# Where a seven-product feed-forward stage makes its weight sums, operand sums and squares

## The chip, the cores and the metric

The kernel runs on one core of a Trainium2 chip. The metric is the device time of one execution in microseconds (us); lower is better. Engines are named as in the profile: PE is TensorE, DVE is VectorE, ACT is ScalarE, POOL is GpSimd, SP is SyncE, which here only issues DMAs. All data is float32; a matmul operand is split into a high part (type fp32r) and a low part, so that one float32 product is three matmuls: high by high, high by low, low by high.

## What is computed

One step of a decoder trunk of two layers, for 512 prompt rows and 32 sample rows (NT = 544 columns; everything is kept transposed, features on partitions):

```python
for i in range(DEPTH):                     # DEPTH = 2, D_MODEL = 1024, D_FF = 2816
    x = x + 0.5 * swiglu(rmsnorm(x, norm_ff1[i]), ffn1_gate[i], ffn1_up[i], ffn1_down[i])
    x = x + (mlstm if i % 2 == 0 else chunk_mlp)(rmsnorm(x, norm_mix[i]))
    x = x + 0.5 * swiglu(rmsnorm(x, norm_ff2[i]), ffn2_gate[i], ffn2_up[i], ffn2_down[i])
y = rmsnorm(x, norm_final)

def swiglu(x, gate, up, down):
    return (silu(x @ gate) * (x @ up)) @ down
```

The states of the mLSTM (matrix memory, normaliser, stabiliser, convolution rows) and the chunk MLP's rows are outputs too. The change touches none of that.

## The kernel before, in words

The kernel has six stages in order: ffn1 of layer 0, the mLSTM, ffn2 of layer 0, ffn1 of layer 1, the chunk MLP, ffn2 of layer 1. The first and the last (`ffn_seven`, L565) work on 2x2 blocks with seven products in place of eight, in the manner of Strassen and Winograd; the other four are plain. The change is in the two seven-product stages and in what prepares their operand.

**Units.** A stage is a list of units (class `Unit`, L172). A unit is one 256-column slab of a weight matrix, stored as four blocks (12, 11, 21, 22). `gated(j)` makes two blocks of gate rows, `hidden(j)` two blocks of up rows and multiplies by the gate, `lowered(m, ...)` adds two rows of blocks of the down projection to x. The list is gated 0, hidden 0, gated 1, hidden 1, gated 2, hidden 2, gated 3, four lowered units over hidden 0 to 2, and so on in groups of three (`SV_GROUPS`, L48). Indices 0, 9 and 10 of gate and up (`EIGHT`, L49) and the last four lowered units have eight products and need no sums. A gated or hidden unit of seven products has 7 x 12 = 84 matmuls, a lowered one 63, each 128x128 by 128x272.

**Sums of weights.** The seven products need, besides blocks 11, 12 and 22, the sums called "7", "5", "6" and "3". "7" and "5" are made by accumulating DMAs that POOL issues onto loaded blocks (`u_add`, L421, parts "7" and "5"). "6" is "7" plus block 22, and "3" is "6" plus block 12 (tile rawd): two adds on POOL. `u_split` then makes high and low parts in halves "a" (12, 11), "b" (6, 7), "c" (5, 22) and "d" (3): ACT copies into the high part, DVE subtracts for the low part (`split_into`, L273). The raw loads rotate over six buffers, three a unit, so that the load of the unit after next takes the buffers of the unit at hand; high and low parts of "a" and "b" rotate over two, those of "c" and "d" have one each, and so has rawd.

**Sums of the operand.** The operand of gate and up (the scaled x; four pairs of row tiles) has eight blocks a pair: B11, B21, B22, B12 and four sums T4, T1, T2, T3. `sums_x` (L394) scales two tiles into tile hT (two ACT copies), splits the first four blocks, makes the sums on DVE (`sums`, L386) and splits those. `prep_sq` (L302) squares a tile of x on ACT and adds it to `acc` on POOL, for the RMS norm; `prep_end` (L312) sums acc over partitions on PE and makes rstd.

**What sets the order.** Within a seven-product stage `self.nc` is an `Ordered` wrapper (L166): on every engine the instructions keep the order in which the program issues them, so one that waits holds back all behind it on its engine. `u_run` (L477) is that order. With u the unit at hand, v the next, w the one after and p the one before, an iteration issues, for a unit of seven products:

- product 11 into bank 0 and ACT's negated copy into bank 2
- loads "a" and "b" of w on SP, the accumulating DMA "7" of w on POOL
- split "c" of u; load "c" of w; the accumulating DMA "5" of w
- the last product ("3") of p, then p's eviction on DVE
- product 12; split "d" of u (reads rawd); split "a" of v
- product 6; ACT's copy of bank 2 into bank 3; `p.then(0)` (ACT's Silu and POOL's product of the gate with rstd, or a part of the hidden split)
- product 7 and its copy to tile e; `p.then(1)`
- adds "6" of w and "3" of v on POOL; split "b" of v
- products 22 (into bank 2) and 5 (into bank 3), and ACT's copy of bank 3 into bank 1

The stage's front (L649 to L664) splits the first unit's weights and, in the first stage, prepares x pair by pair; in the last stage x is prepared by the loop of the chunk MLP's output projection (L1447), outside the Ordered wrapper. Unit 0 runs pair by pair (`wide`), and `prep_end` sits in its iteration.

## Time and profile before

| what | value |
|---|---|
| time, median of 3 runs | 2431.47 us (2431.13 to 2433.59) |
| the profiled execution's own time | 2430.62 us |
| its span, first to last instruction | 2428.9 us |
| PE busy | 2295.4 us (95%), 17504 matmuls |
| DVE busy | 1417.8 us (58%) |
| ACT busy | 958.5 us (39%) |
| POOL busy | 590.4 us (24%) |
| mean granted PE clock | 0.981 of full speed |
| HBM | 154 GB/s over the span |

Times in the rows count from the span's start. A busy share is an average over stages with different limits; matmuls overlap in the pipeline, so that a busy PE is not PE at its peak. The clock granted to PE has two levels, 1.2 and 2.4 GHz; a mean of 1.00 says that it was at the upper one throughout. "x <- y" behind a wait says what ended it. In the tables of instructions, a helper's line stands for all that it issues: in the two Ordered stages everything has L157 (the wrapper's call), so the names of the tiles tell operations apart: raw (loaded weights; on POOL the add "6" or the issue of an accumulating DMA), rawd (the add "3"), whi/wlo (halves "a" and "b"), whc/wlc ("c"), whd/wld ("d"), set (a unit's four banks), hT, xsh/xsl, s, acc, sq.

### The profile page before, as it was taken

The numbers are of one execution on the slowest core, as the hardware profiler recorded it, in microseconds if no ns is written. First come the engines' busy times: TensorE is split into PE (matmuls) and PEld (weight loads), VectorE is DVE, ScalarE is ACT, GpSimd is POOL, SyncE is SP. The second block draws the span as 40 slices with busy tenths as digits, with TensorE's granted clock in tenths as the row PEclk, the third lists the DMA queues.
The fourth block names the chain that finished last, engine by engine and source line by source line (L and its number), as shares of the span: only waits on it lengthen the run. The fifth ranks groups of instructions, "written<-read, shape, count | busy, mean of one in ns | idle before, by whom it ended". The sixth has DMA issues, their size and how long they took to land.

```text
span 2428.9 us, 42264 instructions
## 1 busy us (share of the span) xinstructions
PE 2295.4 (95%) x17504; PEld 2183.5 (90%) x17504; DVE 1417.8 (58%) x1909; ACT 958.5 (39%) x1410; POOL 590.4 (24%) x612
## 2 busy tenths in 40 slices
PE   6988899899999999999999999999999989888997
PEld 5888899888887888999999999999999988888897
DVE  5868685754436666745444455545344667677764
ACT  5535453343535444521222342222244444444443
POOL 3444431334201100210111121011120024444421
PEclk8999999999999999999999999999999999998998
DMA  4555553367676663448463445647232225555541
GB/s 137 137 137 137 138 141 110 112 196 231 206 275 225 222 228 127 155 152 280 165 207 124 128 153 167 242 156 237 84 114 80 72 74 127 130 144 132 149 121 53
DMA packets 158600, 376.85 MB, mean 155 GB/s; under 512 B 16224, under 2 KB 40624, under 8 KB 158408
## 3 DMA queue, kind: packets, MB, share of 16 engines
q1 hardware_dynamic: 112528, 289.66, 36.4%
q0 software_dynamic: 25328, 60.24, 11.5%
q10 hardware_dynamic: 20552, 24.26, 2.8%
q8 instruction: 137, 2.24, 0.4%
q14 instruction: 55, 0.45, 0.1%
HBM read 314.29 MB, written 59.81 MB: 154 GB/s over the span
## 4 chain that ended last, share of the span: by engine, by line
PE 74%; DVE 7%; issue 6%; POOL 6%; DMA 4%; ACT 2%; SPq 0%; POOLq 0%; ACTq 0%; DVEq 0%
PE mm L262 49%; PE set L157 13%; POOL raw L157 3%; DVE hT L157 2%; POOL rawd L157 2%; PE mm L1316 2%; PE s L1109 2%; PE s L1243 1%; PE s L1279 1%; DMA raw<-in_ffn_gate 1%; DMA raw<-in_ffn_up 1%; PE s L887 1%; PE s L262 1%; PE mm L700 1%; DVE wlc L157 1%
## 5 line engine op out<-in xcount | busy, mean ns | idle before, releaser
L276 ACT ACTIVATE whi<-raw 128x1024 fp32r<-128x1024 f32 (+2 forms) x216 | 221.9, 1027 | 751.1 <-PE mm L262 644.9
L262 PE MATMUL mm<-xgh,whi 128*128 128x272 f32 x2368 | 494.8, 290 | 0.2 <-DVE x L1350 0.2
L262 PE MATMUL mm<-xgl,whi 128*128 128x272 f32 x2368 | 490.2, 288 | 0.0
L262 PE MATMUL mm<-xgh,wlo 128*128 128x272 f32 x2368 | 489.8, 288 | 0.0
L262 PEld LDWEIGHTS mm<-xgh,whi 128*128 128x128 f32 x2368 | 372.1, 188 | 18.5 <-issue 14.5
L262 PEld LDWEIGHTS mm<-xgl,whi 128*128 128x128 f32 x2368 | 371.4, 188 | 0.4 <-DVE xgl L157 0.2
L262 PEld LDWEIGHTS mm<-xgh,wlo 128*128 128x128 f32 x2368 | 371.1, 188 | 0.5 <-issue 0.5
L277 DVE TENSOR_TENSOR wlo<-raw,whi 128x1024 fp32r<-128x1024 f32 (+2 forms) x216 | 257.7, 1193 | 46.8 <-ACT whi L276 39.7
L157 DVE TENSOR_TENSOR wlc<-raw,whc 128x1024 fp32r<-128x1024 f32 (+2 forms) x72 | 149.3, 2074 | 183.2 <-ACT whc L157 139.8
L157 PE MATMUL set<-xsh,whi 128*128 128x272 f32 x704 | 207.3, 295 | 15.5 <-ACT xsh L157 13.9
L157 PE MATMUL set<-xsh,wlo 128*128 128x272 f32 x704 | 207.0, 294 | 5.7 <-DVE wlo L157 5.7
L157 PE MATMUL set<-xsl,whi 128*128 128x272 f32 x704 | 207.3, 294 | 2.4 <-DVE xsl L157 2.4
L157 PE MATMUL set<-xsh,whc 128*128 128x272 f32 x448 | 137.0, 306 | 41.1 <-ACT set L157 33.8
L262 PE MATMUL mm<-hh,whi 128*128 128x272 f32 x832 | 173.0, 290 | 0.0
L262 PE MATMUL mm<-hl,whi 128*128 128x272 f32 x832 | 171.9, 288 | 0.0
L262 PE MATMUL mm<-hh,wlo 128*128 128x272 f32 x832 | 171.6, 288 | 0.0
L157 DVE TENSOR_TENSOR wlo<-raw,whi 128x1024 fp32r<-128x1024 f32 (+2 forms) x128 | 145.3, 1141 | 38.4 <-ACT whi L157 38.4
L355 POOL TENSOR_TENSOR s<-s,rstd 128x544 f32<-128x544 f32 x44 | 76.0, 1727 | 354.9 <-ACT s L354 354.9
L157 PEld LDWEIGHTS set<-xsh,whi 128*128 128x128 f32 x704 | 136.5, 194 | 17.1 <-ACT xsh L157 14.6
L157 PEld LDWEIGHTS set<-xsh,wlo 128*128 128x128 f32 x704 | 136.3, 194 | 6.8 <-DVE wlo L157 6.8
L157 PEld LDWEIGHTS set<-xsl,whi 128*128 128x128 f32 x704 | 136.4, 194 | 3.3 <-DVE xsl L157 3.3
L157 PE MATMUL set<-xsh,wlc 128*128 128x272 f32 x448 | 134.2, 300 | 2.0 <-DVE wlc L157 2.0
(386 smaller groups left out, 4887.1 us busy)
## 6 DMA issues: line engine op xcount, KB each, us to landing
raw<-in_ffn_gate SPq DMA_DIRECT2D x88, 512.0 KB
raw<-in_ffn_up SPq DMA_DIRECT2D x88, 512.0 KB
c<-in_sC SPq DMA_DIRECT2D x64, 512.0 KB
c<-in_sC SPq DMA_DIRECT2D x32, 1024.0 KB
out_Cs<-c POOLq DMA_DIRECT2D x32, 1024.0 KB, 6.0
raw<-in_ffn_down SPq DMA_DIRECT2D x64, 384.0 KB
raw<-in_ml_up SPq DMA_DIRECT2D x32, 512.0 KB
raw<-in_ffn_down SPq DMA_DIRECT2D x32, 512.0 KB
```

Source lines behind the costliest of these rows:

```text
L157: r = f(*args, **kw)
L262: nc.tensor.matmul(out=ps[h], lhsT=w[:, wsl], rhs=x[:, h * HN:(h + 1) * HN], start=k == 0 and q == 0, stop=k == n - 1 and q == 2)
L276: nc.scalar.activation(out=hi, in_=src, func=AF.Copy)
L277: nc.vector.tensor_tensor(out=lo, in0=src, in1=hi.bitcast(F32), op=ALU.subtract)
L355: nc.gpsimd.tensor_tensor(out=s, in0=s, in1=self.rstd, op=ALU.mult)
L700: nc.tensor.matmul(out=ps[:, pi, :HN], lhsT=w[:, w0:w0 + P], rhs=h[pi], start=z == 0, stop=z == 6 * nj - 1)
L887: nc.tensor.matmul(out=ps[:, tt * P:(tt + 1) * P], lhsT=t[:, tt * P:(tt + 1) * P], rhs=wd[w], start=True, stop=True)
L1109: nc.tensor.matmul(out=s["qc"][32 * dt:32 * dt + 32, :], lhsT=self.qpad[:, dt, b, :], rhs=c0[:, dd, :], start=b == 0, stop=b == 7, tile_po ...
L1243: nc.tensor.matmul(out=ps[:, :n], lhsT=kk[:, i * P:(i + 1) * P], rhs=qq[:, i * P:NP], start=z == 0, stop=z == 11)
L1279: nc.tensor.matmul(out=ps, lhsT=s_[:, c], rhs=v_[:, i], start=i == 0 and q == 0, stop=i == T and q == 2)
L1316: nc.tensor.matmul(out=ps, lhsT=kk[:, tt], rhs=vv[:, tt], start=tt == 0 and q == 0, stop=tt == 3 and q == 2)
```

## The change

- The adds "6" and "3" run on DVE in place of POOL, and both for the next unit v; "6" was made for w, one iteration earlier. They are issued before `p.then(1)`.
- Split "b" of v is issued at the end of the iteration, behind products 22 and 5 and their copy.
- `sums_x` has two parts. Part 0 scales two tiles of x and splits the first four blocks; part 1 scales them again, makes the sums and splits those. Part 0 runs where the whole ran before. The four parts 1 are handed to `u_run` as `later` and are issued one at each `step`, thus two in the iteration of unit 0 and two in that of unit 1.
- In the first stage all pairs go through the new loop at the stage's front; in the chunk MLP's loop both squares of a pair are now taken behind the pair's part 0.
- Within the Ordered stages `prep_sq` adds the squares on DVE in place of POOL.
- `u_first` handles the units that it is given, with adds in the order "75"; it is called for units of eight products alone, which have no adds.

```diff
--- before.py
+++ after.py
@@ -293,8 +293,9 @@
     def prep(self, k):
         if self.xkind == "s":
             if k % 2:
-                self.px[k // 2] = self.sums_x(k - 1)
-            self.prep_sq(k)
+                self.sums_x(k - 1, 0)
+                self.prep_sq(k - 1)
+                self.prep_sq(k)
             return
         self.px[k] = self.split(self.xg, "xg", self.x[k], scale=self.col(self.pc + k))
         self.prep_sq(k)
@@ -307,7 +308,8 @@
         else:
             sq = self.com.tile([P, NT], F32, tag="sq", name="sq", bufs=2)
             nc.scalar.activation(out=sq, in_=self.x[k], func=AF.Square, scale=one)
-            (eng or nc.gpsimd).tensor_tensor(out=self.acc, in0=self.acc, in1=sq, op=ALU.add)
+            eng = eng or (nc.vector if isinstance(nc, Ordered) else nc.gpsimd)
+            eng.tensor_tensor(out=self.acc, in0=self.acc, in1=sq, op=ALU.add)
 
     def prep_end(self, sums=None):
         nc = self.nc
@@ -391,19 +393,20 @@
         nc.vector.tensor_tensor(out=t[:, T2], in0=t[:, B22], in1=t[:, T1], op=ALU.subtract)
         nc.vector.tensor_tensor(out=t[:, T4], in0=t[:, B21], in1=t[:, T2], op=ALU.subtract)
 
-    def sums_x(self, k):
+    def sums_x(self, k, part):
 
         nc = self.nc
         t = self.ht.tile([P, 8, HN], F32, tag="hT", name="hT", bufs=1)
-        hi, lo = (self.xg.tile([P, 8, HN], F32R, tag="xs", name=n) for n in ("xsh", "xsl"))
+        if part == 0:
+            self.px[k // 2] = [self.xg.tile([P, 8, HN], F32R, tag="xs", name=n) for n in ("xsh", "xsl")]
         nc.scalar.activation(out=t[:, B11:B12 + 1:B12 - B11], in_=self.v2(self.x[k]), func=AF.Copy,
                              scale=self.col(self.pc + k))
         nc.scalar.activation(out=t[:, B21:B22 + 1], in_=self.v2(self.x[k + 1]), func=AF.Copy,
                              scale=self.col(self.pc + k + 1))
-        self.split_into(hi[:, :4], lo[:, :4], t[:, :4])
-        self.sums(t)
-        self.split_into(hi[:, 4:], lo[:, 4:], t[:, 4:])
-        return hi, lo
+        if part:
+            self.sums(t)
+        c = slice(4 * part, 4 * part + 4)
+        self.split_into(*(x[:, c] for x in self.px[k // 2]), t[:, c])
 
     def u_load(self, u, part):
         nc, n = self.nc, u.src.shape[2]
@@ -426,10 +429,10 @@
         elif part == "5":
             nc.gpsimd.dma_start(out=u.c[:, 0], in_=u.src[:, 3], accum_op=ALU.add)
         elif part == "6":
-            nc.gpsimd.tensor_tensor(out=u.b[:, 0], in0=u.b[:, 1], in1=u.c[:, 1], op=ALU.add)
+            nc.vector.tensor_tensor(out=u.b[:, 0], in0=u.b[:, 1], in1=u.c[:, 1], op=ALU.add)
         else:
             u.d = self.wx.tile([P, 512], F32, tag="rawd", name="rawd", bufs=1)[:, :n]
-            nc.gpsimd.tensor_tensor(out=u.d, in0=u.b[:, 0], in1=u.a[:, 0], op=ALU.add)
+            nc.vector.tensor_tensor(out=u.d, in0=u.b[:, 0], in1=u.a[:, 0], op=ALU.add)
 
     def u_split(self, u, part):
 
@@ -457,12 +460,12 @@
 
     def u_first(self, units):
 
-        for u in units[:2]:
+        for u in units:
             for part in "ac" if u.eight else "abc":
                 self.u_load(u, part)
-        for i, u in enumerate(units[:2]):
+        for u in units:
             if not u.eight:
-                for part in "756" if i else "7563":
+                for part in "75":
                     self.u_add(u, part)
 
     def u_copy(self, out, in_, scale=1.0):
@@ -544,13 +547,10 @@
                 self.u_product(u, 1, "7", T3, True)
                 u.e = self.wx.tile([P, HN], F32, tag="e", name="e", bufs=1)
                 self.u_copy(u.e, u.bank[1], u.scale)
+            if v and not v.eight:
+                self.u_add(v, "6")
+                self.u_add(v, "3")
             step(p, 1)
-            if w and not w.eight:
-                self.u_add(w, "6")
-            if v and not v.eight:
-                self.u_add(v, "3")
-            if v and not v.eight:
-                self.u_split(v, "b")
             if u.eight and not wide:
                 self.u_product(u, 2, "22", B21)
                 self.u_product(u, 3, "22", B22)
@@ -558,6 +558,8 @@
                 self.u_product(u, 2, "22", T4)
                 self.u_product(u, 3, "5", T1)
                 self.u_copy(u.bank[1], u.bank[3], -1.0)
+            if v and not v.eight:
+                self.u_split(v, "b")
         self.u_close(units[-1])
         units[-1].then(0)
         units[-1].then(1)
@@ -652,16 +654,18 @@
                 for k in range(2, KD):
                     self.nc.sync.dma_start(out=self.x[k], in_=a["xT"][k])
                 self.u_first(units[1:2])
-                self.u_split(units[0], "a")
-                for k in range(KD):
-                    self.prep(k)
-                    if k == 1:
+                for k in range(0, KD, 2):
+                    self.sums_x(k, 0)
+                    if k == 0:
+                        self.u_split(units[0], "a")
                         self.u_split(units[0], "c")
+                    self.prep_sq(k)
+                    self.prep_sq(k + 1)
             else:
-                self.u_first(units)
+                self.u_first(units[:2])
                 self.u_split(units[0], "a")
                 self.u_split(units[0], "c")
-            self.u_run(units, halt)
+            self.u_run(units, halt, [lambda k=k: self.sums_x(k, 1) for k in range(0, KD, 2)])
             self.nc = nc
             if nextc is None:
                 j0, j1 = SV_GROUPS[-1]
```

## Rows read from the trace of the kernel before

**Rows 1.** the profile's page, part 4: the chain that ended last, by engine
```profile
PE 74%; DVE 7%; issue 6%; POOL 6%; DMA 4%; ACT 2%; SPq 0%; POOLq 0%; ACTq 0%; DVEq 0%
```

**Rows 2.** busy us by stretch (instructions), granted clock, DMA share, GB/s
```profile
62.20:365.20 303.00, 265.94 (x1993) 259.50 (x1994) 226.07 (x223) 142.24 (x228) 131.25 (x108) 0.97 0.56 139
365.20:433.90 68.70, 65.35 (x506) 64.71 (x504) 32.53 (x38) 21.06 (x34) 11.87 (x10) 0.98 0.35 99
475.00:1978.00 1503.00, 1500.44 (x11643) 1409.65 (x11642) 798.76 (x1213) 549.63 (x773) 251.50 (x322) 1.00 0.53 174
2015.50:2322.30 306.80, 269.56 (x1996) 263.36 (x1997) 222.45 (x223) 142.10 (x228) 129.17 (x108) 0.96 0.55 137
2322.30:2387.00 64.70, 61.16 (x484) 60.51 (x482) 32.88 (x38) 20.83 (x34) 11.65 (x9) 1.00 0.36 107
```

**Rows 3.** the chain in order of time, chunk MLP: start us, us
```profile
1929.23 48.07 PE mm L262 x384
```

**Rows 4.** TensorE waits, two stretches: total us, times, longest us
```profile
PE set L157 <- ACT set L157: 31.7, 21, 3.7
PE set L157 <- DVE wlo L157: 5.6, 5, 1.1
...
PE set L157 <- ACT set L157: 34.2, 20, 3.8
PE set L157 <- DVE wlo L157: 3.4, 3, 1.1
```

**Rows 5.** the chain in order of time, 134 to 162: start, us, what
```profile
133.66 0.95 POOL rawd L157
...
135.89 0.29 ACT set L157
...
136.23 2.44 PE set L157 x10
...
147.19 4.78 DMA raw<-in_ffn_up
```

**Rows 6.** groups by form, 62 to 365: busy us, mean ns, idle before
```profile
L157 POOL TENSOR_TENSOR s<-s,rstd 128x1088 f32<-128x1088 f32 x8 | 23.1, 2893 | 0.0
...
L157 DVE TENSOR_TENSOR wld<-rawd,whd 128x512 fp32r<-128x512 f32 x16 | 11.0, 687 | 1.4 <-ACT whd L157 1.2
```

**Rows 7.** DMA issues by line: count, KB each, median us to landing
```profile
raw<-in_ffn_gate POOLq DMA_DIRECT2D x32, 256.0 KB, 4.8
```

**Rows 8.** VectorE timeline, two units: start us, us, operation, [idle before]
```profile
83.91 5.33 DVE L157 TENSOR_TENSOR wlc<-raw,whc 128x1024 fp32r<-128x1024 f32 x1 [2.76 <-PE set L157]
89.16 0.71 DVE L157 TENSOR_TENSOR hT<-set,s 128x544 f32<-128x544 f32 x1
...
96.75 1.22 DVE L157 TENSOR_TENSOR wlo<-raw,whi 128x1024 fp32r<-128x1024 f32 x1
...
100.13 0.71 DVE L157 TENSOR_TENSOR s<-set,rstd 128x544 f32<-128x544 f32 x1
...
103.00 1.23 DVE L157 TENSOR_TENSOR wlo<-raw,whi 128x1024 fp32r<-128x1024 f32 x1 [0.17 <-ACT whi L157]
105.54 1.23 DVE L157 TENSOR_TENSOR wlo<-raw,whi 128x1024 fp32r<-128x1024 f32 x1 [1.31 <-ACT whi L157]
```

**Rows 9.** timelines of ScalarE, then VectorE, in the first opening
```profile
34.51 1.39 ACT L157 ACTIVATE hT<-x,cols 128x544 f32<-128x544 f32 x2 [0.26 <-DVE xsl L157]
...
39.99 1.11 ACT L157 ACTIVATE xsh<-hT 128x1088 fp32r<-128x1088 f32 x1 [2.95 <-DVE hT L157]
...
37.07 1.29 DVE L157 TENSOR_TENSOR xsl<-hT,xsh 128x1088 fp32r<-128x1088 f32 x1 [2.60 <-ACT xsh L157]
38.28 1.67 DVE L157 TENSOR_TENSOR hT<-hT 128x544 f32<-128x544 f32 x3
...
46.35 3.56 DVE L157 RECIPROCAL rstd<-rstd 128x272 f32<-128x272 f32 x2 [1.00 <-ACT rstd L157]
```

**Rows 10.** who waited for whom, whole span: total us, times, longest us
```profile
PE s L320 <- DVE sql L277: 5.8, 1, 5.8
```

## The prediction

> **What bounds the kernel now.** I read the chain of waits first: the kernel ends by TensorE for 74% of the span, but GpSimd stands in the chain with 6%, though it computes little [rows 1]. Then the busy time by stretch. The middle of the span (the xLSTM block, the plain feed-forward stages and the chunk MLP) is TensorE at full rate and the change leaves it alone. The two stages with seven products are different [rows 2]. A matmul of this shape costs 48.07 / 384 = 0.1252 us where nothing stops TensorE [rows 3]. The four stretches behind the openings take 303.0 + 68.7 + 306.8 + 64.7 = 743.2 us for 1993 + 506 + 1996 + 484 = 4979 matmuls [rows 2], which at that rate are 623.4 us. So **119.8 us** are lost there, and this is all that the steady part of the change can win.
>
> Who is late: in the two long stretches TensorE waits 31.7 + 34.2 us for a ScalarE copy of a bank and 5.6 + 3.4 us for the low part of a split weight, 74.9 us [rows 4]. The other 45 us are what follows a stall: the clock granted falls to its lower level of 1.2 GHz (mean 0.97 and 0.96 of 2.4 GHz in those stretches against 1.00 in others [rows 2]) and the stream of matmuls has to fill again. The copy (bank 2 to bank 3) is not slow itself. The chain in order of time shows it: GpSimd ends "rawd" (the sum "3" of this unit's weights) at 134.61, only then can ScalarE split it ("whd") and, behind that in its queue, the next unit's "a" half, and at 135.89 the copy; TensorE goes on at 136.23 [rows 5]. In an earlier unit of the same kind whd waits for rawd as well: the sum sits on GpSimd behind the product of the gate with rstd (2.89 us each [rows 6]) and behind the sum "6" of the unit after, which waits for an accumulating DMA. Further, the load of the unit after next goes into the buffer that rawd reads: the chain runs from rawd into SP and a load of 4.78 us [rows 5], then an accumulating DMA of 4.8 us [rows 7], and back into "6" and "3". It is a loop of about 11 us per unit, longer than a unit's matmuls: 84 x 0.1252 = 10.5 us (gate and up), 63 x 0.1252 = 7.9 us (down). A stage has 28 such units: 8 gate, 8 up, 12 down.
>
> **The change, part by part.**
> (1) *Sums on VectorE, for the next unit.* Both sums of unit v are made in the unit before it, from DMAs issued one unit earlier still, and whd finds its input ready. The buffers of "a" come free in the unit before, so the loop is cut: load 4.78 + accumulate 4.8 = 9.6 us from load to landing, and the first reader stands about 10.5 + 8 = 18 us after the load. That is a margin of 8 us, 5 for down units. SP has only these loads queued; on GpSimd the accumulating issues come earlier and the gate product stands behind the second.
> Price of a sum on VectorE: the trace before has none. The nearest row is wld, two SBUF inputs of 128x512 float32, 0.69 us [rows 6]; above, twice 1024 columns under contention took 5.33 [rows 8], so at most 2.7; below it can't be nothing. I take 0.69, the same form. A unit that evicts a hidden block keeps VectorE busy from 89.16 to the end of its last split, 96.75 + 1.22 = 97.97, 8.8 us, and with an unhindered wlc (1.2, as the other splits) 10.0; one that evicts a gate block takes 2.7 from 100.13 to 103.00 without the wait, and three splits, 3.6, in all 6.3 [rows 8]. Both with two sums each: 16.3 + 2.8 = 19.1 us against 21.0 of TensorE. Down units: three splits at 3/4 (2.6), wld 0.5, eviction 2.0, sums 1.0, in all 6.1 of 7.9. So VectorE fits, and TensorE should set the pace.
> (2) *Split "b" moved behind the last product.* On ScalarE it now waits for the end of the unit (a copy of 0.4 us first): split and low part are ready about 2.5 us into the next unit, after a hidden eviction 3.4 us. The product that needs it begins after 36 matmuls, 4.5 us (27 matmuls, 3.4 us, for down). It is hidden with 1 to 2 us in hand, and with nothing where a hidden eviction stands ahead of the first down unit (three times a stage).
> (3) *What is left of contention.* The split wlc took 5.33 us at 83.91 where its like takes 1.23 [rows 8], while GpSimd worked without a pause. The gate product (2.89 us, once in two units [rows 6]) stays on GpSimd. Where it meets only VectorE's work from PSUM or its idle time it costs nothing; all in the way, it makes 19.1 + 2.9 = 22.0 us of 21.0, 1.0 over. By hand I find it mostly in VectorE's idle time behind the sums of a unit that evicts a gate block.
> The Trainium skill ("SBUF — State Buffer", Who interferes with whom) says that a VectorE instruction with two SBUF inputs and a GpSimd instruction that reads SBUF exclude each other for a whole instruction, whichever starts first; the trace agrees with its 5.33 us. By it the new sums would themselves be blocked by the gate product, 1.0 us over per pair of units and 8 pairs a stage, an estimated 16 us in all; by the idle time just named, nothing.
> So of the 119.8 us I leave 15%, 18 us, for single stalls where (2) and (3) have little in hand: **-102 us**.
> (4) *Opening of the first stage.* In each of four pairs of rows the second half goes: ScalarE waits 2.95 us for the sums and works 1.11 [rows 9], 4.06 us. Three stand ahead of the last first half, which now ends at 38.4 - 12.2 = 26 us. The four second halves come back within the first two units, one after the other for they share one buffer: scaled copy 1.39, sums 1.67, high 1.11, low 1.29 [rows 9], 5.5 us each, 21.8 us; beside them on VectorE the two reciprocals, 3.6 us [rows 9], and four splits of weights, 4.9 us. That makes 56.5 us for the first product that needs the sums. Before, that one begins 12 matmuls behind 62.20, at 63.7. **-7 us**; bounds: -16 (nothing comes back) and +6 (21.8 - 16 if units 0 and 1 hide none).
> (5) *Opening of the last stage.* The second half of the last pair, 4.06 us, leaves its front, with up to 3 more if the clock then stays up; but all four halves, 21.8 us, three of which lay under the chunk MLP, now lie in units 0 and 1, whose 192 matmuls last 24 us. I take **0**, between -7 and +5 (one half uncovered).
> (6) *Squares on VectorE.* Two times seven adds, taken at the 0.69 of a sum: at the opening beside ScalarE's work, in the last four down units beside 48 x 0.1252 = 6 us of matmuls each. At the start of the xLSTM block TensorE waits 5.8 us for sql [rows 10], which stands behind gate weights in VectorE's order, not behind the sum of squares: **0**, from -5.8 to +1.4 (two adds in that row).
> Sum: -102 - 7 = -109. The profiled execution took 2430.62 us (2428.9 span and 1.7 around it), 0.85 under the median of the runs: 2431.5 - 109 = **2322 us**.
>
> **Rivals.**
> *A, VectorE becomes the bound.* With the gate product all in its way a pair takes 22.0 us, and its units' waits for ScalarE's splits (0.17 and 1.31 us after a gate block [rows 8]) 1.5 more: 23.5 in place of 21.0, so 2.5 x 16 pairs = 40 us stay of the 119.8: 2431.5 - 80 - 7 = 2345. For it: VectorE is busy 226 of 303 us already [rows 2]. Against: part of that is time blocked by GpSimd.
> *B, the next late thing takes half.* The moved split "b" comes late by a little in every unit, as wlo does now in some (5.6 us, [rows 4]), and each stall costs clock again: half the 119.8 stays: 2431.5 - 60 - 5 = 2367. Against: 1 to 2 us in hand.
> *C, slower.* The sum "6" on VectorE waits for its accumulating DMA, and behind it in order stand splits and evictions. It decides where the DMA path of 9.6 us grows beyond 18 and by more than 119.8 / 56 units = 2.1 us. At 2.8 late it gives 56 x 0.7 = +39: 2470. Against: DMA is busy 0.56 [rows 2], and a faster pace raises that to some 0.66 only.
> *D, no change.* The copy is late for another reason, rawd being only what the profile names last: 2431. Against: the chain from rawd to TensorE closes within 1.6 us [rows 5].
>
> **How the numbers follow.** Forecast 0.58, A 0.20, B 0.13, C 0.05, D 0.04. Faster by over 0.2% (4.9 us, what a measurement of this kernel can tell from none) are the first three, 0.91; D is 0.04 the same, C 0.05 slower. The low end is the whole 119.8 with 13 of the openings, 2298; the high end takes in A and B with 18 us for their unknown prices, 2385.
>
> **What would show it.** Right: no wait of whd for rawd; TensorE's waits for the ScalarE copy in the long stretches under 15 us of 66; 84 matmuls from start to start in 10.6 to 11 us and down units in 8 to 8.5; a granted clock of 1.00 there; GpSimd with one product a pair and DMA issues alone; product "6" of unit 2 near 56 us. Wrong: VectorE without idle time in these stretches and TensorE waiting for low parts (A, B), or VectorE's sums waiting for DMAs (C).

## The result and the profile after

| what | before | after |
|---|---|---|
| time, median | 2431.68 us (2431.13 to 2433.59, 4 runs) | 2322.24 us (2320.39 to 2324.36, 4 runs) |
| ratio | | 0.9549, 95% interval 0.9532 to 0.9565 |
| the profiled execution, its span | 2430.62, 2428.9 us | 2321.94, 2320.2 us |
| PE, DVE, ACT, POOL busy | 95%, 58%, 39%, 24% | 97%, 61%, 42%, 18% |
| mean granted PE clock | 0.981 | 0.989 |

The time is the one forecast (2322 us). First the chain that ended last, by engine, from the page of the changed kernel; it answers to [rows 1]:

```profile
PE 91%; DVE 4%; ACT 2%; issue 1%; DMA 1%; POOL 0%; SPq 0%; ACTq 0%; POOLq 0%; DVEq 0%
```

GpSimd has gone from the chain, and TensorE holds 91% of it in place of 74%. Next the same stretches as [rows 2], cut at the same matmuls by count (columns: stretch, length, busy us and instructions of PE, PEld, DVE, ACT and POOL, granted clock, DMA share, GB/s):

```profile
55.89:311.35 255.46, 253.59 (x1991) 252.14 (x1992) 223.07 (x274) 147.00 (x228) 62.44 (x57) 0.99 0.69 162
311.35:376.76 65.41, 63.73 (x507) 63.30 (x506) 34.61 (x44) 22.11 (x37) 7.64 (x5) 1.00 0.38 105
408.65:1914.34 1505.69, 1500.41 (x11638) 1409.44 (x11636) 795.88 (x1242) 549.01 (x775) 244.49 (x322) 1.00 0.53 173
1959.77:2216.34 256.57, 253.85 (x1996) 252.85 (x1996) 223.03 (x274) 147.41 (x228) 63.26 (x58) 0.99 0.69 162
2216.34:2279.28 62.94, 61.00 (x486) 60.56 (x484) 34.63 (x44) 21.72 (x36) 7.22 (x5) 1.00 0.38 109
```

A long stretch takes 255 us in place of 303, at a clock of 0.99 in place of 0.97. VectorE's 223 us of work fill 87% of it, against 75% before. The waits of TensorE in the two long stretches (total us, times, longest us) answer to [rows 4]:

```profile
PE set L157 <- ACT set L157: 9.4, 2, 8.9
PE set L157 <- DVE wlo L157: 1.3, 2, 0.9
...
PE set L157 <- ACT set L157: 7.9, 2, 7.4
PE set L157 <- DVE wlo L157: 2.2, 2, 1.3
```

Each first row has one long wait, 8.9 and 7.4 us, at the very start of the stretch: it belongs to the opening. Without these two, 1.0 us of the 65.9 us of waits for the ScalarE copy is left.

**Where the 108.7 us went.** I put the two traces side by side, counted the matmuls, and took the difference of start times (after less before) from border to border:

| part of the program | us |
|---|---|
| first stage, to product 12 of unit 2 (62.20 before, 55.89 after) | -6.3 |
| first stage, the rest | -51.1 |
| start of the xLSTM block, past its first waits (to 487.1 before, 424.9 after) | -4.8 |
| the middle | -0.6 |
| last stage, to product 12 of unit 2 | +7.1 |
| last stage, the rest | -52.6 |
| the end | -0.4 |

The two steady parts are -103.7 together. The openings and the start of the xLSTM block come to -4.6 with the middle, and the prediction's errors in them have opposite signs.

The border in the xLSTM block lies past its first waits, because 16 matmuls change places there between the two kernels (see e4_pool_squares). The border at product 12 of unit 2 has a flaw. In the changed kernel it lies right behind a long wait of TensorE, and the clock is then at its lower level: 12 matmuls take 2.89 us there and 1.62 before (columns as above, first the changed kernel, then the one before).

```profile
55.89:58.78 2.89, 2.89 (x13) 2.89 (x14) 2.89 (x5) 1.44 (x2) 0.00 (x0) 0.50 0.17 47
```

```profile
62.20:63.82 1.62, 1.62 (x13) 1.62 (x13) 0.68 (x1) 1.43 (x2) 0.45 (x1) 1.00 0.11 10
```

So a part of what the openings cost stands in "the rest". Counted 24 matmuls later the first stage is -4.9 and -52.5, the last +8.9 and -54.4, and the steady parts are -106.9 together. The figures of single runs below go by product 12; those of kernels whose openings end in such a wait move in the same way, by up to 5 us for both stages together.

### The profile page after: what moved, and what is told of

Its sections match the earlier page's. It is cut to its first block, busy times and chain, and to the rows that moved or that the text cites. A ratio compares the mean times of both kernels' runs of the same rounds, so it can differ in the third digit from the quotient of the medians.

```text
span 2320.2 us, 42244 instructions
## 1 busy us (share of the span) xinstructions
PE 2260.4 (97%) x17504; PEld 2159.6 (93%) x17504; DVE 1424.9 (61%) x2035; ACT 979.3 (42%) x1426; POOL 413.0 (18%) x486
## 4 chain that ended last, share of the span: by engine, by line
PE 91%; DVE 4%; ACT 2%; issue 1%; DMA 1%; POOL 0%; SPq 0%; ACTq 0%; POOLq 0%; DVEq 0%
PE mm L262 51%; PE set L157 27%; PE mm L1320 2%; PE s L1113 2%; PE s L1247 1%; PE s L1283 1%; PE s L891 1%; PE mm L704 1%; PE s L262 1%; DVE wlo L157 1%; DVE hT L157 1%; PE s L1506 1%; PE s L1230 1%; ACT hT L157 0%; PE s L1434 0%
## 5 line engine op out<-in xcount | busy, mean ns | idle before, releaser
L276 ACT ACTIVATE whi<-raw 128x1024 fp32r<-128x1024 f32 (+2 forms) x216 | 222.0, 1028 | 761.6 <-PE mm L262 655.6
L277 DVE TENSOR_TENSOR wlo<-raw,whi 128x1024 fp32r<-128x1024 f32 (+2 forms) x216 | 256.1, 1186 | 44.4 <-ACT whi L276 38.0
L157 PE MATMUL set<-xsh,whi 128*128 128x272 f32 x704 | 207.8, 295 | 21.8 <-ACT set L157 16.3
L157 DVE TENSOR_TENSOR wlo<-raw,whi 128x1024 fp32r<-128x1024 f32 (+2 forms) x128 | 161.5, 1261 | 47.9 <-ACT whi L157 47.8
L157 ACT ACTIVATE whi<-raw 128x1024 fp32r<-128x1024 f32 (+2 forms) x128 | 123.3, 963 | 50.9 <-PE set L157 37.1
L262 PEld LDWEIGHTS mm<-hh,whi 128*128 128x128 f32 x832 | 130.1, 188 | 4.5 <-issue 4.4
```

The source lines that it names most:

```text
L157: r = f(*args, **kw)
L262: nc.tensor.matmul(out=ps[h], lhsT=w[:, wsl], rhs=x[:, h * HN:(h + 1) * HN], start=k == 0 and q == 0, stop=k == n - 1 and q == 2)
L276: nc.scalar.activation(out=hi, in_=src, func=AF.Copy)
L277: nc.vector.tensor_tensor(out=lo, in0=src, in1=hi.bitcast(F32), op=ALU.subtract)
```

## The experiments

Each starts from the changed kernel unless it says otherwise. "The changed kernel" has 2322.2 us throughout; the kernel before had medians from 2428.6 to 2431.7 in the different sessions, so that differences of a few us between kernels of different sessions are uncertain by some 3 us. A time without a ratio beside it comes from a single run.

### Engine and place, one at a time

Both sums on GpSimd, in the new unit and place (e1_pool_sums):

```diff
-            nc.vector.tensor_tensor(out=u.b[:, 0], in0=u.b[:, 1], in1=u.c[:, 1], op=ALU.add)
+            nc.gpsimd.tensor_tensor(out=u.b[:, 0], in0=u.b[:, 1], in1=u.c[:, 1], op=ALU.add)
...
-            nc.vector.tensor_tensor(out=u.d, in0=u.b[:, 0], in1=u.a[:, 0], op=ALU.add)
+            nc.gpsimd.tensor_tensor(out=u.d, in0=u.b[:, 0], in1=u.a[:, 0], op=ALU.add)
```

> The changed kernel (2322 us) with both weight sums put back on GpSimd, in the new place (for the next unit, ahead of the second half-step). Theory 'loop cut, TensorE sets the pace': the place cuts the loop, and VectorE is needed only because GpSimd's adds would block it: whd no longer waits for rawd, but four adds of 1.3 to 1.8 us per pair of units join the gate product's 2.9 us on the shared access to SBUF, 8 to 10 us against the 2 us that VectorE has spare, so 2340 to 2390. Rival 'place alone': GpSimd does as well there, 2322 within 6. Rival 'engine alone': the gain came from VectorE doing the sums, so it goes back above 2410.

Measured: **2422.2 us**. Of the 103.7 us of the steady parts 11 are left, 5.6 in each stage. My theory had the place as the larger half, and that fell. GpSimd in one pair of units of this kernel, as its timeline (start us, us, operation, [idle before and what ended it]):

```profile
101.36 0.87 POOL L157 DMA_DIRECT2D raw<-in_ffn_down  x1 [5.17 <-DVE s L157]
103.37 0.83 POOL L157 DMA_DIRECT2D raw<-in_ffn_down  x1 [1.14 <-DVE wlo L157]
103.93 2.86 POOL L157 TENSOR_TENSOR s<-s,rstd 128x1088 f32<-128x1088 f32 x1
106.43 1.58 POOL L157 TENSOR_TENSOR raw<-raw 128x512 f32<-128x512 f32 x1
108.09 1.27 POOL L157 TENSOR_TENSOR rawd<-raw 128x512 f32<-128x512 f32 x1
```

The two sums of the next unit (raw and rawd) stand behind two issues of accumulating DMAs of the unit after, which are released late (5.17 and 1.14 us of idle time), and behind the gate product. They take 1.58 and 1.27 us; VectorE takes 0.69 for each.

The reverse, both sums on VectorE in the old units and the old place (e2_dve_old_place):

```diff
-            if v and not v.eight:
-                self.u_add(v, "6")
-                self.u_add(v, "3")
             step(p, 1)
+            if w and not w.eight:
+                self.u_add(w, "6")
+            if v and not v.eight:
+                self.u_add(v, "3")
```

> The changed kernel with both sums on VectorE, but for the old units and at the old place ('6' for the unit after next, '3' for the next, behind the second half-step). Theory 'loop cut': the loop load, accumulating DMA, '6', '3', next load is closed again (4.8 + 4.8 + 1.4 and the split, over 11 us per unit against 10.5 and 7.9 of matmuls), and now VectorE's queue stands behind the DMA: 2400 to 2480, VectorE's '6' waiting for DMAs by microseconds in most units. Rival 'engine alone': 2322 to 2335. Rival 'place alone': as before the change, 2425 to 2435.

Measured: **2384.3 us**; -22.5 and -23.8 in the steady parts. The engine alone is worth 46 of the 104 us, and the theory's "2400 or more" was too dark. What is missing shows in this kernel's waits between 80 and 300 us (total us, times, longest us):

```profile
DVE raw L157 <- DMA raw<-in_ffn_up: 29.2, 7, 5.4
ACT whd L157 <- DVE rawd L157: 25.4, 18, 3.6
...
DVE raw L157 <- DMA raw<-in_ffn_down: 18.3, 6, 3.7
PE set L157 <- DVE wlo L157: 16.6, 14, 3.1
```

The sum "6" of the unit after next now waits on VectorE for its accumulating DMA, and splits stand behind it. That is the mechanism of my rival C. In the changed kernel, where the sum is made one unit later, VectorE's sums wait 1.3 us for DMAs in the same stretch.

### What held GpSimd's sums back

The edit of the first experiment, and with it gpsimd replaced by vector in the gate's product with rstd (e10_pool_sums_dve_gate):

> The changed kernel with both weight sums back on GpSimd (as in e1_pool_sums, 2422 us) and the gate product on VectorE, so that the sums no longer share GpSimd with it. In the trace of e1_pool_sums the two sums take 1.6 + 1.5 us on GpSimd, and GpSimd begins them only when the issues of the two accumulating DMAs of the unit after, which stand ahead of them in its queue, have been released; the gate product stood ahead of them once in two units. Theory 'queue order' (the issues that wait for loads and buffers hold the sums back, the gate product adds 2.9 us in every other unit): the issues stay, so most of the loss stays: 2385 to 2410. Rival 'the gate product on GpSimd is what made e1_pool_sums late': 2310 to 2350. Rival 'GpSimd's sums keep VectorE out, whatever else GpSimd does': VectorE takes 2.9 us of product on top and the time stays at 2415 to 2435.

Measured: **2374.7 us**, between the bands of two theories: moving the gate product gave back 48 of the 100 us that GpSimd's sums cost. Not all of that need be the lateness of these sums: in the changed kernel, which has no sums on GpSimd, the same move gains 12.6 us (e8_gate_on_dve, below).

The other suspect, with sums and gate product all on GpSimd: the accumulating DMAs of the unit after are issued behind the sums (e13_pool_sums_first).

```diff
                 if not w.eight:
                     self.u_load(w, "b")
-                    self.u_add(w, "7")
...
                 self.u_load(w, "c")
-                if not w.eight:
-                    self.u_add(w, "5")
...
                 self.u_add(v, "3")
+            if w and not w.eight:
+                self.u_add(w, "7")
+                self.u_add(w, "5")
             step(p, 1)
```

> As e1_pool_sums (both weight sums on GpSimd, gate product on GpSimd too), with one thing else: the two accumulating DMAs of the unit after are issued behind the two sums and no longer ahead of them, so that nothing that waits for a load stands before a sum in GpSimd's queue. Theory 'queue order' (e1_pool_sums lost because its sums stood behind issues that wait): the sums then begin when VectorE's did, take 3.1 us in place of 1.4, and what remains is GpSimd's own time and the time for which it keeps VectorE out: 2340 to 2375. Rival 'GpSimd is too slow or blocks VectorE, wherever its sums stand': 2400 to 2430. Rival 'the accumulating DMAs now land late' (issued half a unit later, margin 8 us less some 5): TensorE waits for split "c" or for the sums again, over 2375, with waits for these DMAs in the trace.

Measured: **2347.1 us**, as queue order foretold. GpSimd's timeline for the same pair of units:

```profile
97.91 2.89 POOL L157 TENSOR_TENSOR s<-s,rstd 128x1088 f32<-128x1088 f32 x1 [5.92 <-ACT s L157]
100.77 1.28 POOL L157 TENSOR_TENSOR raw<-raw 128x512 f32<-128x512 f32 x1
102.13 1.29 POOL L157 TENSOR_TENSOR rawd<-raw 128x512 f32<-128x512 f32 x1
103.35 1.74 POOL L157 DMA_DIRECT2D raw<-in_ffn_down  x2
```

No issue that waits for a load precedes a sum, and 75 of the 100 us are back without any work leaving GpSimd. The two remedies (48 and 75) add up to more than 100, so they cure in part the same lateness. But the accumulating DMAs, issued later, now land late, and the sums themselves wait for them (all engines' waits, 80 to 300 us):

```profile
POOL raw L157 <- DMA raw<-in_ffn_up: 32.8, 7, 5.7
...
POOL raw L157 <- DMA raw<-in_ffn_down: 17.8, 6, 4.1
```

That is the second rival's mechanism, though the time is not over its 2375. What separates 2347 from 2322 is this wait, GpSimd's slower sums, the gate product ahead of them, or the time for which GpSimd keeps VectorE out; the four were not told apart.

The gate product alone, moved to VectorE in the kernel **before** (e12_before_dve_gate):

> The kernel before with one word changed: the gate product on VectorE, and everything else (sums on GpSimd in the old units and places, whole operand sums, squares on GpSimd) as it was. GpSimd loses 2.89 us per pair of units, the loop from rawd over SP's load and the accumulating DMA back into the sums stays at some 11 us. Theory 'the loop sets the pace, the gate product only lengthens it where it stands ahead of a sum': about a quarter of the steady loss goes, 2390 to 2415. Rival 'the gate product ahead of the sums is the whole lateness': the 104 us of the change come with this word alone, 2325 to 2350. Rival 'no part of it, the loop alone': 2420 to 2432.

Measured: **2412.6 us**, ratio 0.9929 (0.9913 to 0.9946), -8.6 and -8.1 in the steady parts. whd still waits for GpSimd's rawd, 73.7 us in all between 80 and 300 us (57.9 in the kernel before). So the one word is worth 16 us and the loop stays, as the theory said.

### How near VectorE is to its limit

Each sum issued twice (e6_sums_twice):

```diff
             nc.vector.tensor_tensor(out=u.b[:, 0], in0=u.b[:, 1], in1=u.c[:, 1], op=ALU.add)
+            nc.vector.tensor_tensor(out=u.b[:, 0], in0=u.b[:, 1], in1=u.c[:, 1], op=ALU.add)
```

(and the same for the other sum)

> The changed kernel with each of the two weight sums issued twice on VectorE (the second instruction makes the same values again), so that VectorE has 4 x 0.69 = 2.8 us more in a pair of a gate and an up unit and 2 x 0.55 = 1.1 more in a down unit. By the working of the prediction a pair goes from 19.1 to 21.9 us of VectorE against 21.0 of TensorE, 0.9 over: 16 pairs x 0.9 = 14 us, and with the clock lost at each stall up to 25: 2336 to 2347, with TensorE waiting for low parts on VectorE. Rival 'VectorE has room' (waits of TensorE do not grow, since work is only shifted inside idle time and the splits of the next unit are made early enough): 2322 to 2328. Rival 'VectorE already sets the pace' (the prediction's rival A): the whole 4 x 0.69 x 16 = 44 us and the down units' 24 x 1.1 = 26 on top: over 2380.

Measured: **2361.3 us**, 39 more, where 14 to 25 were expected. In the second full pair of a gate and an up unit (168 matmuls, 89.62 to 114.13 here, 86.10 to 107.23 in the changed kernel) VectorE is busy 24.1 of 24.5 us; in the changed kernel 20.9 of 21.1. My 19.1 was too low, and VectorE's timeline in the changed kernel shows by what:

```profile
94.77 0.69 DVE L157 TENSOR_TENSOR raw<-raw 128x512 f32<-128x512 f32 x1
95.49 3.31 DVE L157 TENSOR_TENSOR rawd<-raw 128x512 f32<-128x512 f32 x1
```

and GpSimd's in the same microseconds:

```profile
95.40 2.84 POOL L157 TENSOR_TENSOR s<-s,rstd 128x1088 f32<-128x1088 f32 x1
```

The sum rawd takes 3.31 us where its twin before it takes 0.69: the gate product began at 95.40 and ended at 98.24, and the sum ended at 98.80, 0.56 us later. The prediction had found the gate product "mostly in VectorE's idle time behind the sums"; in this pair it falls on the second sum, and the mean of the wide rawd sums between 80 and 300 us is 1.14 us.

The gate product on VectorE in every unit (e8_gate_on_dve):

```diff
-                        self.nc.gpsimd.tensor_tensor(out=g, in0=g, op=ALU.mult,
+                        self.nc.vector.tensor_tensor(out=g, in0=g, op=ALU.mult,
```

> The changed kernel with the product of the gate with rstd on VectorE in every unit, so that GpSimd computes nothing in the two seven-product stages and only issues DMAs. In the trace of the changed kernel the sum rawd takes 1.08 us on the mean in place of 0.69 and single ones 3.5, beside the gate product. Theory 'what is left of contention costs little in the steady part, and at the openings about 3 us each' (the operand's sums took 3.50 us in place of 0.44 there): steady part within 3 us, both openings up to 3 us shorter each, 2315 to 2321. Rival 'it costs nothing that counts': the product on VectorE itself (1088 columns, two SBUF inputs, some 1.3 us by the splits of that width, or more) takes back what it frees: 2321 to 2325. Rival 'contention costs up to 16 us' (the estimate by the lock rule in the prediction): 2306 to 2312.

Measured: **2309.6 us**, ratio 0.9511 (0.9497 to 0.9525). Groups by form in this kernel, 80 to 300 us (busy us, mean ns, idle before):

```profile
L157 DVE TENSOR_TENSOR rawd<-raw 128x512 f32<-128x512 f32 x13 | 9.0, 692 | 0.5
L157 DVE TENSOR_TENSOR s<-s,rstd 128x1088 f32<-128x1088 f32 x7 | 9.0, 1284 | 0.0
```

The same product takes 1.28 us on VectorE and 2.89 on GpSimd [rows 6], and rawd is back at 0.69. So VectorE has less to do with the product than without it: the pair above falls from 20.9 to 19.7 us. Between 80 and 300 us its busy time falls from 195.6 to 191.7 us although seven products (9.0 us) have come to it, so without GpSimd's products the rest of its work takes 12.8 us less. The wide rawd sums account for 5.8 of these (14.8 us against 9.0); most of the rest lies in splits, where the mean of the 128x1024 wlo falls from 1.32 to 1.22 us and that of the 128x768 one from 1.19 to 0.95. Against the changed kernel the steady parts gain 3.2 and 5.0 us (-54.3 and -57.6 in all), the openings 2.9 and 2.1. I had expected 2315 to 2321 and at most 3 us in the steady part; the time lies in the band of the case "up to 16 us", 2306 to 2312.

The Trainium skill ("SBUF — State Buffer", Who interferes with whom) has a VectorE instruction with two SBUF inputs and a GpSimd instruction that reads SBUF shut each other out for a whole instruction; the 3.31 us in place of 0.69 agree with it. The estimate of 16 us for the steady parts that the prediction worked out from it, and did not take, stands against 8.2 us that these parts gained in this run.

### The moved split "b"

Split "b" of the next unit back in its old place, right behind the sums (e5_split_b_early):

```diff
             if v and not v.eight:
                 self.u_add(v, "6")
                 self.u_add(v, "3")
+            if v and not v.eight:
+                self.u_split(v, "b")
             step(p, 1)
...
-            if v and not v.eight:
-                self.u_split(v, "b")
         self.u_close(units[-1])
```

> The changed kernel with one part undone: split "b" of the next unit stands right behind the two sums again, ahead of the delayed work of the unit before and of products 22 and 5. In the trace of the changed kernel TensorE still waits for the low part at the first down unit of each group, six times in all, 0.43 + 0.88 + 1.35 + 0.90 + 1.29 + 1.18 = 6.0 us. My theory (the move of split b costs just these stalls, because nothing is in hand there): they go, and the time is 2316 to 2320. Rival 'the move is needed': ScalarE waits with this split for the end of product 7 and for the sums, and behind it now stands the second part of the hidden split, which the next units need: more stalls than the six, over 2325. Rival 'the move is worth nothing': 2320 to 2324, with the six stalls still there, since the hidden eviction and not the split is what is late.

Measured: **2329.2 us**, ratio 0.9593 (0.9577 to 0.9609). The stalls at the first down units went, and worse ones came: this theory fell, and the rival "the move is needed" had the time (over 2325) and the engine right, though what came late behind the split was not the hidden split. The wait of ScalarE for the sums, between 80 and 300 us, in this kernel:

```profile
ACT whi L157 <- DVE raw L157: 26.8, 19, 2.4
```

and in the changed kernel:

```profile
ACT whi L157 <- DVE raw L157: 5.2, 6, 1.2
```

Split "b" waits on ScalarE for the sum, and the bank copies behind it come late: at 88.18 the split begins after a wait of 2.19 us, the two copies follow at 89.15 and 89.47, and TensorE, stopped for 0.55 us, goes on at 89.58. It waits 26.6 us in all for such copies here, against 17.4. The move belongs to the sums on VectorE.

### The openings and the squares

Whole operand sums ahead of both stages, as before the change; nothing is handed to the units (e3_whole_sums):

```diff
-                self.sums_x(k - 1, 0)
+                self.sums_x(k - 1, None)
...
-                    self.sums_x(k, 0)
+                    self.sums_x(k, None)
...
-            self.u_run(units, halt, [lambda k=k: self.sums_x(k, 1) for k in range(0, KD, 2)])
+            self.u_run(units, halt)
```

(None makes both parts, one after the other)

> The changed kernel with the operand's sums made whole ahead of each seven-product stage, as before the change (weight sums and squares stay on VectorE). From the traces of before and after, the first opening won 6.3 us and the last lost 7.1. Theory 'the two openings cancel': product 12 of unit 2 in the first stage begins 4 to 8 us later than after the change, in the last stage 5 to 9 us earlier counted from the stage's start, and the time is 2322 within 5. Rival 'the split of the operand's sums carries part of the gain in both openings': 2332 or more. Rival 'the openings lost on the whole': 2312 or less.

Measured: **2312.7 us**, ratio 0.9523 (0.9509 to 0.9537). Against the kernel before, the first opening is -2.7 here and -6.3 with the change; the last one is -2.2 here and +7.1 with it. So the two parts gain 3.6 us in the first stage and lose 9.3 in the last (2.2 and 11.1 when counted behind the low clock), where three of the four pairs had lain under the chunk MLP. The theory that the openings cancel fell; the nearest band is that of the rival "the openings lost on the whole", 2312 or less. In the changed kernel the last of these chains runs so (VectorE's timeline in the first opening):

```profile
43.12 4.75 DVE L157 TENSOR_TENSOR hT<-hT 128x544 f32<-128x544 f32 x3 [1.33 <-ACT hT L157]
49.04 1.29 DVE L157 TENSOR_TENSOR xsl<-hT,xsh 128x1088 fp32r<-128x1088 f32 x1 [1.17 <-ACT xsh L157]
...
51.78 1.68 DVE L157 TENSOR_TENSOR hT<-hT 128x544 f32<-128x544 f32 x3
54.64 1.29 DVE L157 TENSOR_TENSOR xsl<-hT,xsh 128x1088 fp32r<-128x1088 f32 x1 [1.18 <-ACT xsh L157]
```

and ScalarE's, to the copy that TensorE waits for, with TensorE's first matmul behind it:

```profile
53.50 1.11 ACT L157 ACTIVATE xsh<-hT 128x1088 fp32r<-128x1088 f32 x1 [1.75 <-DVE hT L157]
54.51 1.04 ACT L157 ACTIVATE whi<-raw 128x1024 fp32r<-128x1024 f32 x1
55.46 0.38 ACT L157 ACTIVATE set<-set 128x272 f32<-128x272 f32 x1
```

```profile
55.89 0.60 PE L157 MATMUL set<-xsh,whi 128*128 128x272 f32 x1 [8.90 <-ACT set L157]
```

TensorE does not stop for the sums but for the copy of bank 0 to bank 2, which stands behind the four second parts in ScalarE's order. And the third pair's three sums take 4.75 us where the fourth's take 1.68: the gate product of unit 0 runs on GpSimd from 44.22 to 47.07. The last opening shows the same, 4.76 us for the third pair's sums on VectorE and the gate product from 1948.12 on GpSimd:

```profile
1946.98 4.76 DVE L157 TENSOR_TENSOR hT<-hT 128x544 f32<-128x544 f32 x3 [1.33 <-ACT hT L157]
```

```profile
1948.12 2.85 POOL L157 TENSOR_TENSOR s<-s,rstd 128x1088 f32<-128x1088 f32 x1
```

Two parts in the first stage only, with the gate product of unit 0 on VectorE (e9_parts_first_whole_last):

```diff
-                        self.nc.gpsimd.tensor_tensor(out=g, in0=g, op=ALU.mult,
+                        (self.nc.gpsimd if j else self.nc.vector).tensor_tensor(out=g, in0=g, op=ALU.mult,
...
-            self.u_run(units, halt, [lambda k=k: self.sums_x(k, 1) for k in range(0, KD, 2)])
+            self.u_run(units, halt, [lambda k=k: self.sums_x(k, 1) for k in range(0, KD, 2)] if start else ())
```

(and the chunk MLP's loop makes whole sums)

> A version meant to beat the changed kernel and the one with whole operand sums (2312.7): the first stage keeps its operand sums in two parts, the last stage makes them whole under the chunk MLP as before the change, and the gate product of unit 0 alone is on VectorE. From the runs: the split is worth 3.6 us in the first opening against whole sums and costs 9.3 in the last one, so 2322.2 - 9.3 = 2313 without the gate product, or 2312.7 - 3.6 = 2309. With the gate product of unit 0 off GpSimd the operand's sum of 3.50 us in the first opening goes back to about 0.44, 3 us of a chain that TensorE waits 8.9 us for: 2306 to 2310. Rival 'the chain at the first opening is set by the reciprocals or by ScalarE, not by that sum': 2309 to 2313.

Measured: **2308.4 us**, ratio 0.9508 (0.9494 to 0.9522), openings -7.8 and -1.8. Units 0 and 1 leave TensorE 5.8 us of wait for the copy in place of 8.9, the 3 us expected. The first opening gains only 1.5 of them against the changed kernel: TensorE's wait for its first weights, ahead of unit 0, is 6.3 us in this run in place of 5.0.

The squares added by GpSimd again (e4_pool_squares):

```diff
-            eng = eng or (nc.vector if isinstance(nc, Ordered) else nc.gpsimd)
+            eng = eng or nc.gpsimd
```

> The changed kernel with the squares of the seven-product stages added on GpSimd again. From the traces, the stretch between the first stage's last product and the middle of the span got 5.4 us shorter. Theory 'squares': the last sum of squares comes earlier on VectorE, so that stretch gets 4 to 9 us longer again and the time is 2326 to 2331. Rival 'order of VectorE's queue at the border, changed by something else': the stretch stays as after the change and the time is 2322 within 2. In the first opening the squares on GpSimd cost under 2 us by either.

Measured: **2327.1 us**, ratio 0.9584 (0.9563 to 0.9606). The start of the xLSTM block is at -0.4 in place of -4.8: the squares on VectorE are worth 4.4 us there and 5 in the whole. (The middle is at +2.5 in place of -0.6, by steps between 818 and 851 us, where TensorE's order is the same in all three kernels; their cause was not followed.) In the kernel before, GpSimd's timeline at that border says why:

```profile
460.51 2.12 POOL L763 TENSOR_TENSOR wd<-qkv,con 128x128 f32<-128x128 f32 x3
462.60 1.35 POOL L157 TENSOR_TENSOR acc<-acc,sq 128x544 f32<-128x544 f32 x1
```

and ScalarE's of the same kernel:

```profile
463.98 0.66 ACT L276 ACTIVATE sqh<-acc 128x544 fp32r<-128x544 f32 x1 [2.68 <-POOL acc L157]
```

The last add waits on GpSimd behind three products for the next block's weights, and takes 1.35 us; on VectorE it takes 0.92 and stands right behind the split of its row tile. TensorE's waits there go from 5.8 + 1.9 to 3.5 + 0.4 us. Its timelines show a second thing (kernel before, then the changed one):

```profile
464.69 0.52 PE L320 MATMUL s<-sqh,onesr 128*128 128x272 f32 x2 [1.87 <-ACT sqh L276]
...
472.50 0.82 PE L320 MATMUL s<-sql,onesr 128*128 128x272 f32 x2 [5.78 <-DVE sql L277]
```

```profile
405.40 0.53 PE L322 MATMUL s<-sqh,onesr 128*128 128x272 f32 x2 [0.42 <-ACT sqh L276]
...
412.98 0.39 PE L322 MATMUL s<-sql,onesr 128*128 128x272 f32 x1 [3.54 <-DVE sql L277]
```

The low part sql comes 7.8 and 7.6 us behind the high part, hardly sooner. But TensorE's order has changed with the squares: 28 matmuls stand between the two in the changed kernel, and 12 in the kernel before and in this run. So 16 matmuls that had stood behind the wait run ahead of it. The earlier sqh brings about 1.5 us of the 4.8, and the rest comes with this order.

### All together

The gate product on VectorE in every unit and two parts in the first stage only (e11_all_together):

> A version meant to beat all before it: the gate product on VectorE in every unit (2309.6 on the changed kernel) and whole operand sums under the chunk MLP in the last stage, with sums in two parts in the first stage only (2308.4 with the gate product of unit 0 alone on VectorE). The last opening cost +5.0 us against the kernel before in the run with all gate products on VectorE and -1.8 with whole sums: 2309.6 - 6.8 = 2303, range 2300 to 2306. Rival 'the two gains are the same one' (the last opening was cured by the gate product of unit 0, not by the whole sums): 2307 to 2310.

Measured: **2302.4 us** (2301.4 to 2305.3), ratio 0.9482 (0.9468 to 0.9496), in the range expected. This is the fastest version, 16 us (by the ratios) to 20 us (by the medians) under the changed kernel. The steady parts of this kernel (80 to 300 us, columns as in the table of stretches):

```profile
80.00:300.00 220.00, 219.92 (x1751) 219.70 (x1749) 191.67 (x247) 127.09 (x197) 37.55 (x45) 1.00 0.70 167
```

TensorE has no idle time left in these 220 us. The steady parts gain 54.9 + 59.0 = 113.9 of the 119.8 us that the prediction had counted as lost.

## Why the prediction was right, and where it was not

- **What bounds it, and how much there is to win: right.** 119.8 us were counted, and a kernel without stalls wins 113.9 of them. Most signs named in advance came: in the first long stretch whd waits for rawd once, 0.4 us, and in the last not at all; the ScalarE copy costs 1.0 of 66 us, a pair of gate and up units takes 21.1 us (10.6 each), a down unit 8.1, the clock between 80 and 300 us is 1.00 (0.99 in the long stretches with their openings' low clock). Product "6" of unit 2 starts at 58.8 us and not near 56. The 45 us that were put down to the clock and to filling the stream again were not split: by the granted clocks of [rows 2] some 23 of them can be the clock's.
- **(1) to (3), -102: measured -103.7** (-106.9 behind the low clock). The two parts of (1) had to come together: engine alone -46, place alone -11, both -104. The price of a sum, 0.69 us, is exact (0.685 on the mean). The margin at the DMA held: between 80 and 300 us the sums wait 1.3 us for it.
- **(2): right in size, not in reason.** The six stalls at the first down units of a group came, 0.4 to 1.4 us each, 6.0 in all. That the move itself buys something, 7 us, I had not seen: it keeps ScalarE's bank copies from standing behind a wait for the sums.
- **(3): the wrong side.** "Mostly in VectorE's idle time" failed: the gate product falls on the sum rawd, where it costs 2.6 us, and on splits. VectorE then has 20.9 us in the pair shown, not 19.1, of 21.1, so that rival A was only 0.2 us away. The steady cost, 8 us by e8_gate_on_dve, was covered by the 18 us kept back for single stalls, and so the sum still came out.
- **(4), -7: measured -6.3** at product 12, and -5.0 at product "6", for which the sum was made (58.8 us against 56.5, and 63.8 before). That the length of the chain came out near is in part luck: that the sums would be kept out for 3 us at their worst place was not in it, and neither was the low clock behind the wait. What TensorE waits for is the copy behind the sums.
- **(5), 0 between -7 and +5: measured +7.1** (+8.9 behind the low clock). This term failed, beyond its bound. The working priced the part that leaves the front and trusted 24 us of matmuls to hide 21.8 us of halves. But they start only behind unit 0's own evictions, and one is kept out for 3 us.
- **(6), 0 at the xLSTM block, from -5.8 to +1.4: measured -4.8,** inside its bounds. The step that failed is "not behind the sum of squares": sql stands in VectorE's order, but sqh, ahead of it, waited 2.68 us for GpSimd's last add. The row read was the longer of two waits; the shorter one, in front of it, was not looked at. That TensorE's order would change there, which brings the larger part, was not foreseen either.
- The errors, +7.1 in (5) against -4.8 in (6) and -1.7 in (1) to (3), cancel to within 1 us. That the total meets the forecast to 0.2 us is luck; the terms (1) to (3), which make nearly all of it, are within 2 us (5 behind the low clock).

## What to carry to other kernels

An add moved off a slow engine pays in full only if its inputs have landed when the new engine comes to it: move the engine and the place in the order together, and look at what stands ahead of it in the old queue, DMA issues included, for a reordering there gave 75 of the 100 us. Before work that GpSimd does beside a busy VectorE is called hidden, look for the VectorE instruction that starts while it runs; moving that work onto VectorE itself may lighten VectorE. Work taken out of a stage's front is free only where the stage behind has room, and must be priced anew for each stage: the same split gained 2 to 4 us in one and lost 9 to 11 in the other.

## What the runs showed of the hardware

The same elementwise product of 128x1088 float32 took 2.89 us on GpSimd and 1.28 on VectorE. A VectorE sum of 0.69 us that started 0.09 us behind it took 3.31 and ended 0.56 us after GpSimd's product, so one product on GpSimd cost VectorE 2.6 us, twice what the product costs on VectorE. A stall also costs clock: behind TensorE's wait of 8.9 us the granted clock was 0.50 of the upper level (1.2 of 2.4 GHz), and 12 matmuls took 2.89 us against 1.62. With 75 us of waits in the two long stretches the clock was 0.97 and 0.96, and without them its mean is 1.00 between 80 and 300 us.
